# Streaming encoder step: input norm and the first three projections, interleaved block by block in five PSUM banks, with the bias rows spread once

## The chip, the core and the metric

The kernel runs on one core of a Trainium2 chip. Five engines work side by side, each on its own queue in program order: TensorE (PE, matmuls; PEld is its weight load), VectorE (DVE), ScalarE (ACT), GpSimd (POOL) and SyncE (SP), which here only issues DMAs. ACT issues DMAs too (its queue's rows are called ACTq). The metric is the device time of one execution in microseconds.

## What is computed

One inference step of two layers on 1024 prompt frames and 64 sample frames (1088 columns together), D = 1024. The part that matters is the start of layer 0: an RMS norm of the input and the first rows of the big input projection, for the first pair of attention heads.

```python
def rmsnorm(x, g):
    y = xf * lax.rsqrt(jnp.mean(xf * xf, axis=-1, keepdims=True) + EPS)
    return y * g
def mixer_even(h, conv_hist, ck, cv, w_in, conv_w, table, w_out):
    p = h @ w_in
    a_b, a_c, a_h, a_z, q, k, v, b_z = jnp.split(p, 8, axis=-1)
    ...
    o, nk, nv = band_attn_prompt(q, k, v, table)      # or band_attn_sample with the cache ck, cv
    ...
idx = jnp.clip(q_pos[:, None] - k_pos[None, :], -REL_CLIP, REL_CLIP) + REL_CLIP
bias = jnp.take(table, idx, axis=1)                   # added to the attention scores
```

## The kernel before

All activations lie transposed: channels on the 128 partitions in KT = 8 blocks, frames along the free axis in three groups of 384, 384 and 320 columns (`GROUPS`). Every fp32 product is made of three passes in a fast format: an operand is split into a rounded part `hi` (a copy on ACT) and the rest `lo` (a subtraction, mostly on DVE), and a projection adds w_hi·h_hi + w_hi·h_lo + w_lo·h_hi over the 8 blocks, so 24 matmuls for one weight tile and one group (`project`, line 174). The split weights are `whi`, `wlo` (`stage`, `split`, lines 147 to 164), the split normed input of group g is `hhi`, `hlo`. `project` writes one PSUM bank (`pjt`), taken from a pool of two by `bank`; an eviction (`ev_v`, `ev_q`, `ev_k`, `ev_z`) then copies it out.

`start` (line 353) does the input norm and the projections v, q, k (weights 0, 1, 2) of head pair 0. It squares the input blocks on ACT (line 377), adds the squares into `sqa` (line 379, on DVE for groups 0 and 1, on POOL for group 2), sums over partitions by one fp32 matmul with a constant (`rstd`, line 196), takes the root as exp(-0.5 ln) on ACT (lines 201, 202), and builds each normed block with three instructions (`h_tile`, lines 215 to 217): DVE makes `hf` = x · gain · rstd in SBUF, ACT rounds it to `hhi`, and DVE or POOL subtracts to get `hlo`. Group 0 is normed first. Then weight 0 runs over group 0; weight 1 over group 0, and the root of group 1 with its eight blocks; weight 2 over group 0, and the root of group 2 with its blocks. Groups 1 and 2 follow, weight by weight. A weight's tiles are given back by `drop` after its last group, which lets the next weight be staged; up to three are held. Below, "z" is the fourth projection of the pair (weight 3, line 654), and the first matmul of weight 4 follows it.

The bias table is needed as 128 shifted rows. `Lt` (line 639) is a short row for each of 8 heads, stored to DRAM as `Ld`; for each head `v_tokens` copies it 128 times to `Gd` (line 504) and reads it back at a slant as `bias` (line 506), all on ACT's DMA queue. The cached keys `ck` (line 445) share a buffer with the key output `ko` (tag "ko"), and are split in `split_k` directly after they are loaded (line 446).

What stands where in an engine's queue is decided at build time: the generators of `Order` set the order in which PE's work is written (`yield` lets attention units of a head pair in between), and the scheduler of the tile framework arranges each engine's instructions from that.

## Time and profile before

| what | us |
|---|---|
| median of 3 runs | 1475.85 (1473.38 to 1477.38) |
| the profiled execution | 1476.87 |
| its span, first to last instruction | 1475.1 |
| PE busy in the span | 1371.8 (93%) |
| DVE / ACT / POOL busy | 884.4 / 681.4 / 314.3 |
| mean granted TensorE clock | 0.98 |

Rows of a timeline give the start in us, the duration, the engine (ACTq and SPq rows are DMA issues), the line, the operation, out<-in, the shape, and in brackets how long the engine sat idle before it and what ended that. The duration of a matmul counts its way through the array, so that back-to-back matmuls overlap: their cost is the distance between starts. Rows of a window give for each engine the busy us and, in brackets, its number of instructions.

### The profile page before, as it was taken

Reading aid. Unit: us, or ns where it says so; the run is one execution under the profiler, and the core shown is the slowest. Engines: PE = TensorE matmul, PEld = TensorE weight load, DVE = VectorE, ACT = ScalarE, POOL = GpSimd, SP = SyncE. Lnnn points to the kernel's source line nnn. Section 1 sums busy time; section 2 is a strip of 40 time slices with the busy share of each in tenths; the row PEclk is TensorE's granted clock in tenths of the full one; section 3 lists DMA queues with packets and bytes.
Section 4 is the critical chain, followed back from the end, with each engine's and each line's share of the span. In section 5 each row is a group of like instructions: output and inputs, shape, how many; then the busy total and the mean of one; then the engine's idle time right before and its main releaser. Section 6 shows DMA issues by size and latency. Waiting matters only on the chain. (4 is left out here: it accounts for less than half of the span.)

```text
span 1475.1 us, 28417 instructions
## 1 busy us (share of the span) xinstructions
PE 1371.8 (93%) x10578; PEld 1233.6 (84%) x10578; DVE 884.4 (60%) x2496; ACT 681.4 (46%) x1780; POOL 314.3 (21%) x813
## 2 busy tenths in 40 slices
PE   4999999999999999989878999999999989998995
PEld 3888998999899899878867777878887877888985
DVE  6647237425624855768687767666766656443654
ACT  6544144234424446775455553544443534323642
POOL 4100000000000012341136224240424152210332
PEclk9999999999999999999999999999999999999998
DMA  5231210211121164551432222122211232347454
GB/s 204 63 136 44 78 59 26 78 61 45 53 70 58 34 216 137 181 186 60 85 98 69 40 43 61 35 42 48 70 33 41 61 87 70 92 122 229 150 188 157
DMA packets 114378, 133.12 MB, mean 90 GB/s; under 512 B 35568, under 2 KB 81336, under 8 KB 114240
## 3 DMA queue, kind: packets, MB, share of 16 engines
q1 hardware_dynamic: 82128, 101.86, 24.2%
q10 hardware_dynamic: 32112, 29.45, 6.1%
q8 instruction: 83, 1.36, 0.4%
q14 instruction: 55, 0.45, 0.1%
HBM read 99.91 MB, written 34.51 MB: 91 GB/s over the span
## 5 line engine op out<-in xcount | busy, mean ns | idle before, releaser
L119 PE MATMUL pjt<-hhi,wlo 128*128 128x384 f32 (+1 forms) x1768 | 620.8, 351 | 2.5 <-DVE wlo L164 2.4
L119 PE MATMUL pjt<-hhi,whi 128*128 128x384 f32 (+1 forms) x1768 | 586.7, 332 | 19.5 <-ACT whi L163 4.1
L119 PE MATMUL pjt<-hlo,whi 128*128 128x384 f32 (+1 forms) x1768 | 585.9, 331 | 7.3 <-DVE hlo L217 6.6
L119 PEld LDWEIGHTS pjt<-hhi,whi 128*128 128x128 f32 x1768 | 339.5, 192 | 29.5 <-ACT hhi L216 6.6
L119 PEld LDWEIGHTS pjt<-hhi,wlo 128*128 128x128 f32 x1768 | 339.9, 192 | 27.5 <-issue 12.4
L119 PEld LDWEIGHTS pjt<-hlo,whi 128*128 128x128 f32 x1768 | 338.4, 191 | 10.5 <-DVE hlo L217 8.8
L164 DVE TENSOR_TENSOR wlo<-wf,whi 128x512 fp32r<-128x512 f32 x222 | 155.8, 727 | 144.7 <-ACT whi L163 143.0
L163 ACT CAST whi<-wf 128x512 fp32r<-128x512 f32 x222 | 130.0, 619 | 160.5 <-PE pjt L119 113.0
L546 ACT ACTIVATE pr<-pr,mx 128x640 f32<-128x640 f32 (+5 forms) x72 | 50.9, 707 | 92.7 <-DVE mx L545 92.2
L721 DVE SCALAR_TENSOR_TENSOR kq<-pjt,par,kq 128x384 f32<-128x384 f32 (+2 forms) x144 | 71.6, 497 | 2.9
L347 POOL TENSOR_TENSOR sqa<-sqa,sq 128x384 f32<-128x384 f32 (+1 forms) x36 | 37.9, 1052 | 154.0 <-ACT sq L345 153.9
L507 POOL MEMSET bias<- 64x64 f32 x8 | 1.4, 178 | 313.1 <-DMA bias<-Gd 312.6
L543 DVE CUSTOM_DVE_ANT_0 pr<-sc,bias 128x640 f32<-128x640 f32 (+5 forms) x72 | 48.0, 666 | 26.3 <-PE sc L119 22.8
L928 POOL TENSOR_TENSOR px<-AL 48x14 f32<-48x14 f32 (+6 forms) x168 | 45.1, 269 | 61.3 <-DMA AL<-Sd 52.2
L1091 DVE SCALAR_TENSOR_TENSOR S<-S,egl,su 128x128 f32<-128x128 f32 x128 | 40.6, 343 | 28.9 <-PE su L119 28.5
L692 POOL TENSOR_TENSOR so<-so 128x4 f32<-128x4 f32 (+2 forms) x72 | 16.8, 233 | 176.7 <-DVE so L685 117.9
L882 ACT ACTIVATE junk<-tr 128x128 f32<-128x128 f32 x136 | 37.7, 277 | 34.9 <-PE tr L124 29.5
L929 POOL TENSOR_TENSOR AL<-AL,px 48x14 f32<-48x14 f32 (+6 forms) x168 | 46.7, 278 | 9.4
L119 PE MATMUL pjt<-mhi,whi 128*128 128x384 f32 x128 | 43.9, 343 | 4.9 <-ACT mhi L163 4.9
L124 PE MATMUL pt<-cst,pr 128*128 128x128 f32 (+1 forms) x280 | 43.2, 269 | 4.4 <-DVE pr L548 2.9
L1050 ACT ACTIVATE junk<-o 128x128 f32<-128x128 f32 x68 | 21.0, 309 | 51.9 <-DVE o L1046 43.1
L119 PE MATMUL pjt<-mlo,whi 128*128 128x384 f32 x128 | 43.9, 343 | 0.0
(238 smaller groups left out, 2208.5 us busy)
## 6 DMA issues: line engine op xcount, KB each, us to landing
wf<-in_w_in SPq DMA_DIRECT2D x128, 256.0 KB, 3.3
wf<-in_w_out SPq DMA_DIRECT2D x96, 256.0 KB, 3.3
mf<-mixd SPq DMA_DIRECT2D x32, 192.0 KB, 3.2
x<-in_x SPq DMA_DIRECT2D x8, 384.0 KB, 5.4
xg<-in_x SPq DMA_DIRECT2D x2, 1536.0 KB
xd<-xg SPq DMA_DIRECT2D x2, 1536.0 KB, 6.9
Dd<-dbuf ACTq DMA_DIRECT2D x16, 192.0 KB, 2.7
od<-o ACTq DMA_DIRECT2D x12, 256.0 KB, 3.4
```

The costliest lines, as they stand in the source:

```text
L119: return self.pe.matmul(out, lhsT=lhsT, rhs=rhs, start=start, stop=stop, **k)
L124: return self.pe.transpose(out, in_, self.ident[0:k, 0:k])
L163: self.act.copy(out=hi, in_=x)
L164: (eng or self.dve).tensor_tensor(lo, x, hi.bitcast(F32), ALU.subtract)
L347: pool.tensor_tensor(acc, acc, sq, ALU.add)
L543: dve.tensor_tensor_reduce(out=cut(pr[0:nq, :nk]), in0=sc[0:nq, :nk // nw, :nw], in1=cut(b["bias"][a][0:nq, j0:j0 + nk]), scale=1.0, scala ...
L546: act.activation(pr[0:nq, :nk], pr[0:nq, :nk], AF.Exp, bias=mx[0:nq, 1:2], scale=1.0, accum_out=mx[0:nq, 2:3])
L721: dve.scalar_tensor_tensor(oi, ch(ps[:, i0 + j + 1:i0 + j + 1 + m]), cw[j], oi, ALU.mult, ALU.add)
L882: act.activation(junk, ps[:, i, :], AF.Square, accum_out=ss[:, a, i0 + i:i0 + i + 1])
L928: pool.tensor_tensor(t, AL[:, j + 1:16, j:j + 1].broadcast_to([lanes, m, w]), x.broadcast_to([lanes, m, w]), ALU.mult)
L929: pool.tensor_tensor(o, o, t, ALU.add)
L1091: dve.scalar_tensor_tensor(Sn[:, q, :], S[:, q, :], egl[:, q, p, c:c + 1], su[q], ALU.mult, ALU.add)
```

## The change

`start` is written anew. Its parts, with their names in the diff:

- **Root.** Group 0's eight blocks are squared half on ACT and half on DVE, added in pairs, and the five remaining tiles go through five accumulating fp32 matmuls (`root`). Groups 1 and 2 are squared on ACT, and added on POOL except for the last square, which PE adds. The root goes back into the same PSUM tile (`rr`, one buffer) instead of SBUF, and `hf` lies in PSUM too (two buffers). All `hlo` are made on DVE.
- **Order.** One loop over the groups and, inside, over the 8 blocks: a block is normed some blocks ahead, then all three weights are applied to it (nine matmuls), into three banks at a time out of five. In group 2 only weights 0 and 1 run so, and weight 2 follows as a `project`. The squares of group g+1 are made during the first four blocks of group g, and its root is taken with the sixth.
- **PE fill.** Three fp32 matmuls on constants (`idle`) at the start, two more behind group 0's root; nobody reads them.
- **Staging.** Weights 0 and 1 use the permanent three buffers `wf`, weight 2 two buffers of its own; `cst` is loaded after the input.
- **Bias rows.** `Lt`, `Ld` and all eight `Gd` copies are issued on SP after group 0, `Lt` in the memory of group 0's input.
- **Cached keys.** `ck` has a buffer of its own, is loaded one step earlier for the later pairs, and is split before z.
- The PSUM pools of the attention are opened only after `start`.

```diff
-        return p.tile([P, 512], F32, name="pjt", tag="pj", bufs=2 if p is self.pj else 4)
+        return p.tile([P, 512], F32, name="pjt", tag="pj", bufs=2 if p is self.pj else self.extra)
...
-            wf = (tp if tp and len(self.ready) > 1 else self.wp).tile([P, 4, cols], F32, name="wf", tag="wf", bufs=3)
+            own = not tp or len(self.ready) < 2
+            wf = (self.wp if own else tp).tile([P, 4, cols], F32, name="wf", tag="wf", bufs=3 if own else 2)
...
     def start(self, evs, load):
...
+        pn = self.open("pn", space=PSUM)
+        self.more_banks(3, (0, 1, 0, 1, 1))
...
+        def root(g, parts):
+            n = GROUPS[g][1]
+            ps = pn.tile([P, 512], F32, name="rr", tag="rr", bufs=1)[:, :n]
+            for i, a in enumerate(parts):
+                self.mm(ps, self.meanm, a, i == 0, i == len(parts) - 1)
+            r = tp.tile([P, GMAX], F32, name="rstd", tag="rstd", bufs=1)[:, :n]
+            act.activation(r, ps, AF.Ln, bias=self.eps, scale=1.0)
+            act.activation(ps, r, AF.Exp, scale=-0.5)
+            return ps
+        def block(g, k, r):
...
+            hf = pn.tile([P, 512], F32, name="hf", tag="hf", bufs=2)[:, :n]
+            dve.scalar_tensor_tensor(hf, xs[g][:, k, :], self.par[:, P_PRE + k:P_PRE + k + 1], r, ALU.mult, ALU.mult)
+            act.copy(out=hi[:, k, :], in_=hf)
+            dve.tensor_tensor(lo[:, k, :], hf, hi[:, k, :].bitcast(F32), ALU.subtract)
+        def idle(n):
+            for _ in range(n):
+                self.mm(warm[:, :GMAX], self.meanm, self.eps.broadcast_to([P, GMAX]))
+        warm = self.bank()
+        idle(3)
...
+        r = root(0, parts)
+        idle(2)
+        self.ahead(tp)
+        ws = [self.take() for _ in range(3)]
...
+        for _ in range(3):
+            g, k = todo.pop(0)
+            block(g, k, roots[g])
         for g, (t0, n) in enumerate(GROUPS):
+            hi, lo = self.hops(g)
+            m = 3 if g < 2 else 2
+            ps = [self.bank() for _ in range(m)]
             for k in range(KT):
+                if todo:
+                    block(*todo[0], roots[todo[0][0]])
+                    todo.pop(0)
+                if g < 2:
+                    for j in range(2 * k, min(2 * k + 2, KT)):
+                        sq = square(g + 1, j, "sq" if j else "sqa", 3 if j else 1)
+                        if j == 0:
+                            acc = sq
+                        elif j < KT - 1:
+                            pool.tensor_tensor(acc, acc, sq, ALU.add)
+                    if k == 5:
+                        roots[g + 1] = root(g + 1, [acc, sq])
+                        todo = [(g + 1, i) for i in range(KT)]
+                        block(*todo.pop(0), roots[g + 1])
+                for w, p in zip(ws, ps):
+                    self.mm(p[:, :n], w[0][:, k, :], hi[k], k == 0, False)
+                    self.mm(p[:, :n], w[1][:, k, :], hi[k], False, False)
+                for w, p in zip(ws, ps):
+                    self.mm(p[:, :n], w[0][:, k, :], lo[k], False, k == KT - 1)
+            for i in range(m):
+                evs[i](g, ps[i])
                 if g == 2:
                     self.drop()
+            if g == 0:
+                Lt = tp.tile([8, LROW], F32, name="Lt", tag="x0")
...
+                    nc.sync.dma_start(self.Gd[h], bass.AP(row.tensor, row.offset, [[0, P], [1, LROW]]))
+        p = yield from self.project(ws[2], self.hops(2), GROUPS[2][1])
+        evs[2](2, p)
+        self.drop()
...
             def load():
-                ck = ap.tile([P, CB], F32, name="ck", tag="ko")
-                (nc.scalar if p else nc.sync).dma_start(ck, I["ckT"][p])
-                split_k(ck, [(SEQ, 0, CB)])
+                b["ck"] = ap.tile([P, CB], F32, name="ck", tag="ck")
+                (nc.scalar if p else nc.sync).dma_start(b["ck"], I["ckT"][p])
...
-                nc.scalar.dma_start(self.Gd[h], bass.AP(row.tensor, row.offset, [[0, P], [1, LROW]]))
...
                 if i == 1:
                     yield f"att{p - 1}.8"
                     new_qk()
+                    load()
                     load_v()
-                elif i == 3 and p:
-                    load()
+                elif i == 3:
+                    split_k(B[p]["ck"], [(SEQ, 0, CB)])
```

PE's queue at the first projection, before the change (whi_139 and wlo_140 are weight 0, hhi0 and hlo0 group 0's blocks, pjt_300 the bank):

```order
L119 MATMUL pjt_217<-sqa_194,mean_76 128x384
L119 MATMUL pjt_300<-hhi0_131,whi_139 128x384
L119 MATMUL pjt_300<-hlo0_132,whi_139 128x384
L119 MATMUL pjt_300<-hhi0_131,wlo_140 128x384
L119 MATMUL pjt_300<-hhi0_131,whi_139 128x384
L119 MATMUL pjt_300<-hlo0_132,whi_139 128x384
```

The same place with the change (whi_176, whi_186 and whi_196 are the three weights):

```order
L119 MATMUL rr_165<-s2_157,mean_76 128x384
L119 MATMUL pjt_131<-eps_73,mean_76 128x384 x2
L119 MATMUL pjt_231<-hhi0_159,whi_176 128x384
L119 MATMUL pjt_231<-hhi0_159,wlo_177 128x384
L119 MATMUL pjt_232<-hhi0_159,whi_186 128x384
L119 MATMUL pjt_232<-hhi0_159,wlo_187 128x384
L119 MATMUL pjt_233<-hhi0_159,whi_196 128x384
L119 MATMUL pjt_233<-hhi0_159,wlo_197 128x384
L119 MATMUL pjt_231<-hlo0_160,whi_176 128x384
L119 MATMUL pjt_232<-hlo0_160,whi_186 128x384
L119 MATMUL pjt_233<-hlo0_160,whi_196 128x384
```

Where one normed block fed three matmuls before the next one was needed, it now feeds nine, and `hlo` is asked for after six of them instead of after one.

ACT's queue between the last evictions of group 2 and z, before (Gd, bias and out_vT are DMA issues; whi is a weight's split):

```order
L504 DMA Gd_84<-Ld 128x767
L504 DMA Gd_85<-Ld 128x767
L474 DMA out_vT<-vT 128x576
L504 DMA Gd_86<-Ld 128x767
L453 ACTIVATE qs<-pjt 64x320 x2
L163 CAST whi<-wf 128x512
L506 DMA bias<-Gd_84 128x640
L506 DMA bias<-Gd_85 128x640
L163 CAST whi<-wf 128x512
L504 DMA Gd_87<-Ld 128x767
L504 DMA Gd_88<-Ld 128x767
L504 DMA Gd_89<-Ld 128x767
```

And with the change:

```order
L512 DMA vtok<-in_cv 128x4x128
L572 DMA bias<-Gd_84 128x640
L572 DMA bias<-Gd_85 128x640
L540 COPY vT<-pjt 128x320
L164 CAST whi<-wf 128x512 x2
L521 ACTIVATE qs<-pjt 64x320 x2
L164 CAST whi<-wf 128x512
L542 DMA out_vT<-vT 128x576
L504 CAST ks<-pjt 64x256 x2
L504 CAST ks<-pjt 64x64 x2
L164 CAST whi<-wf 128x512
```

The eight `Gd` issues are gone from ACT's queue (they stand on SP's, behind the weights that are prefetched), and only the two `bias` reads, which wait for `Gd`, are left ahead of the evictions.

ACT's queue in the middle of group 0, with the change (x_129 and x_130 are the inputs of groups 1 and 2; the whi in the middle is the second half of weight 1):

```order
L390 CAST hhi_159<-hf 128x384
L371 ACTIVATE sq<-x_129 128x384
L390 CAST hhi_159<-hf 128x384
L371 ACTIVATE sq<-x_130 128x320
L164 CAST whi<-wf 128x512
L390 CAST hhi_159<-hf 128x384
L371 ACTIVATE sq<-x_130 128x320
L390 CAST hhi_159<-hf 128x384
L504 CAST ks<-ck 64x512 x2
L508 COPY ks<-ks 64x512
L371 ACTIVATE sqa<-x_130 128x320
```

Squares of the next groups, a weight's split and the split of the cached keys stand between the blocks' roundings there.

## The prediction

> **What bounds the kernel now.** I read the page's head first, then windows cut at PE's own milestones, then the timeline of the first 90 us.

> ```profile
> PE 1371.8 (93%) x10578; PEld 1233.6 (84%) x10578; DVE 884.4 (60%) x2496; ACT 681.4 (46%) x1780; POOL 314.3 (21%) x813
> PE   4999999999999999989878999999999989998995
> ```

> PE is the bound nearly everywhere; the first of the 40 slices of PE is the weak one. The cuts below are the first projection matmul (15.03), the end of PE's longest early wait (30.66), the start of z (71.39) and the first matmul of weight 4 (88.60).

> ```profile
> 15.03:30.66 15.63, 8.89 (x19) 5.25 (x19) 15.48 (x20) 11.88 (x25) 10.03 (x9) 1.00 0.53 184
> 30.66:71.39 40.73, 37.37 (x201) 35.30 (x202) 23.33 (x42) 19.85 (x43) 6.44 (x7) 1.00 0.14 34
> 71.39:88.60 17.21, 13.74 (x75) 13.42 (x73) 4.47 (x9) 6.99 (x15) 0.58 (x4) 0.90 0.80 284
> 88.60:1475.10 1386.50, 1310.19 (x10286) 1179.16 (x10284) 832.22 (x2405) 632.27 (x1679) 294.21 (x788) 0.98 0.30 86
> ```

> In the second window DVE is busy 15.48 of 15.63 us: there it bounds, and PE does 19 matmuls. After 88.60 PE is busy 1310.19 of 1386.50, and its order of work there is the same with the change, row for row. So the case is decided by when the first matmul of weight 4 starts, plus what later stalls go or come.

> ```profile
> 15.03 0.69 PE L119 MATMUL pjt<-hhi,whi 128*128 128x384 f32 x1 [3.31 <-ACT hhi L216]
> 16.50 0.52 PE L119 MATMUL pjt<-hhi,whi 128*128 128x384 f32 x1
> 16.82 0.52 PE L119 MATMUL pjt<-hlo,whi 128*128 128x384 f32 x1
> 30.66 0.69 PE L119 MATMUL pjt<-hlo,whi 128*128 128x384 f32 x1 [4.63 <-DVE hlo L217]
> 35.95 0.40 PE L119 MATMUL pjt<-hhi,wlo 128*128 128x384 f32 x1
> 70.95 0.31 PE L119 MATMUL pjt<-hhi,whi 128*128 128x320 f32 x1
> 71.39 0.34 PE L119 MATMUL pjt<-hhi,whi 128*128 128x384 f32 x1
> 75.41 0.34 PE L119 MATMUL pjt<-hhi,wlo 128*128 128x384 f32 x1
> 79.22 0.44 PE L119 MATMUL pjt<-hhi,whi 128*128 128x384 f32 x1 [3.47 <-ACT ko L466]
> ```

> Matmuls overlap, so their price is the distance of starts. At 71.39 the 24 matmuls of z's first group take 23 distances in 4.02 us, 0.175 each; three of 320 columns take 0.44, 0.147 each. At 16.50 the same 384 columns take 0.32: PE runs at half pace. (The granted clock column says 1.00 there; the distances decide.)

> **Term 1, the first block: no gain.**

> ```profile
> 8.24 0.94 ACT L377 ACTIVATE sq<-x 128x384 f32<-128x384 f32 x2 [0.48 <-DMA x<-in_x]
> 10.07 1.65 PE L119 MATMUL pjt<-sqa,mean 128*128 128x384 f32 x2 [10.07 <-DVE sqa L379]
> 11.76 0.58 ACT L201 ACTIVATE rstd<-pjt,eps 128x384 f32<-128x384 f32 x1
> 12.74 0.52 ACT L202 ACTIVATE rstd<-rstd 128x384 f32<-128x384 f32 x1
> 38.27 0.81 PE L119 MATMUL pjt<-sqa,mean 128*128 128x384 f32 x2
> ```

> The last input lands at 8.24. Now two squares of it and the adds follow one another to 10.0; with the change one square is on ACT and one on DVE, done at 8.8. But five fp32 matmuls take the root where one did (a row with x2 is one of them, 1.65 slow, 0.81 fast). Three can start from about 5.5. If the fill matmuls have brought PE to full pace, the last two end at 8.8 + 1.6 = 10.4; if not, five at 1.65 end at 5.5 + 8.3 = 13.8. I take 11.5, near the 11.76 of now. After the logarithm ACT's queue holds three weight roundings, the exponential and the first block: 0.58 + 3 × 0.62 + 0.52 + 0.51 = 3.5 us against 3.27 now (11.76 to 15.03). First block at 15.0, bounds 13.9 to 17.3.

> **Term 2, PE's own work up to z.** 144 matmuls at 0.175 and 72 at 0.147 are 25.2 + 10.6 = 35.8, four root matmuls at 0.81 are 3.2: 39.0. From 15.0 this is a floor of 54.0 for z, against 71.39. It holds if nine matmuls per block (1.6 us) cover what the others do per block.

> ```profile
> L216 ACT CAST hhi<-hf 128x384 fp32r<-128x384 f32 x16 | 8.1, 510 | 3.8 <-DVE hf L215 3.7
> L377 ACT ACTIVATE sq<-x 128x384 f32<-128x384 f32 x14 | 6.9, 516 | 2.0 <-DMA x<-in_x 0.9 <-DVE sqa L379 0.9
> L163 ACT CAST whi<-wf 128x512 fp32r<-128x512 f32 x14 | 8.5, 617 | 7.6 <-PE pjt L119 3.7 <-DMA Gd<-Ld 3.7
> L164 DVE TENSOR_TENSOR wlo<-wf,whi 128x512 fp32r<-128x512 f32 x14 | 10.0, 737 | 8.2 <-ACT whi L163 8.1
> L379 POOL TENSOR_TENSOR sqa<-sqa,sq 128x320 f32<-128x320 f32 x7 | 7.4, 1061 | 1.8 <-ACT sq L377 1.6
> L215 DVE SCALAR_TENSOR_TENSOR hf<-x,par,rstd x24: 537/612/1390, 13.5 to 59.9; 128x384 f32<-128x384 f32 x16, 128x320 f32<-128x320 f32 x8
> L217 DVE TENSOR_TENSOR hlo<-hf,hhi x40: 480/550/1203, 15.1 to 695.8; 128x384 fp32r<-128x384 f32 x26, 128x320 fp32r<-128x320 f32 x14
> L453 ACT ACTIVATE qs<-pjt 64x384 fp32r<-64x384 f32 x4 | 1.9, 486 | 6.0 <-PE pjt L119 5.9
> L456 DVE SCALAR_TENSOR_TENSOR qs<-pjt,qs 64x384 fp32r<-64x384 f32 x4 | 2.2, 555 | 9.1 <-ACT qs L453 9.1
> ```

> DVE per block: 0.61 + 0.55 = 1.16. ACT per block: a rounding and one or two squares, 1.0 to 1.5. POOL: six adds a group, 6.4 us against some 14. On average PE is the longest, but not by much, and the queues are in order. So I count waits one by one:

> - First block: `hlo` is behind two weight subtractions on DVE, some 1.6 us after `hhi`; six matmuls cover 1.0. Wait 0.6.
> - Fifth block: weight 1's second half is rounded only after six block roundings and nine squares: 14.5 + 15 × 0.51 = 22.2, and 0.62 + 0.7 later it is split, 23.5; PE is there at 15.0 + 0.6 + 4 × 1.6 = 22.0. Wait 1.2 or so.
> - First block of group 1: the root's chain (0.58, 0.52, 0.61, 0.51, with squares between: about 5 us) against three blocks, 4.7. With its `hlo`: 0.9.
> - Third and fourth block of group 1: ACT evicts v, q, k of group 0 first (seven pieces at 0.49, 3.4 us), DVE four pieces at 0.555 (2.2). Wait 1.1.
> - Root of group 2: it writes `rr`, which the last `hf` of group 1 still reads. Wait 0.5.
> - Group 2: DVE has 8 × (0.54 + 0.48) + 2.2 = 10.4 us, PE 48 × 0.147 = 7.1, and DVE starts some 2.5 earlier. Wait 1.1.

> Together 5.4; bounds nothing (every chain a little shorter than counted) and 11 (each twice as long). z starts at 59.4, bounds 53 to 66.

> One price rests on `hf` and the root being in PSUM.

> ```profile
> 44.62 1.00 POOL L217 TENSOR_TENSOR hlo<-hf,hhi 128x384 fp32r<-128x384 f32 x1 [10.10 <-ACT hhi L216]
> 44.64 1.39 DVE L215 SCALAR_TENSOR_TENSOR hf<-x,par,rstd 128x384 f32<-128x384 f32 x1
> 737.05 1.20 POOL L839 TENSOR_TENSOR dbuf<-cst,dbuf 128x384 f32<-128x384 f32 x1 [2.62 <-DVE dbuf L836]
> 737.50 1.27 DVE L721 SCALAR_TENSOR_TENSOR vt<-pjt,cwh,vt 128x384 f32<-128x384 f32 x2
> ```

> Beside a POOL instruction `hf` from SBUF took 1.39 where its median is 0.61; the same operation with one operand in PSUM (`pjt`) took 0.64 each beside a longer POOL instruction. I therefore take 0.61 for `hf`, though twelve POOL adds stand beside the blocks; stretched by 0.7 each, they would cost DVE 8.4 us, which is inside rival B. [...]

> **Term 3, z.** From 71.39 to 88.60 are 17.2 us, of which PE's work is 48 × 0.175 + 24 × 0.147 = 11.9. The other 5.3 are the hole from 75.41 to 79.22 and half pace behind it. The hole comes from ACT, which waits in its queue:

> ```profile
> 65.20 0.57 ACTq L504 DMA_DIRECT2D Gd<-Ld  x1
> 70.51 2.71 ACTq L506 DMA_DIRECT2D bias<-Gd  x2
> 73.26 0.62 ACT L163 CAST whi<-wf 128x512 fp32r<-128x512 f32 x1 [3.67 <-DMA Gd<-Ld]
> 75.46 0.76 ACT L434 CAST ks<-pjt 64x256 fp32r<-64x256 f32 x2 [1.58 <-DMA out_vT<-vT]
> 78.74 0.43 ACT L466 COPY ko<-pjt 128x320 f32<-128x320 f32 x1
> ```

> ACT is held until the `Gd` copies land, so k of group 2 is evicted late and z's second group has no bank. With the change the copies go out on SP after group 0, from about 30. Behind them on SP stand only weight loads from the second half of weight 4 on, needed after 77. The first copy now takes 5.3 us (issued at 65.20, the read that waits for it goes at 70.51), so they are there before 40; ACT reaches the reads after 50. What is late next at z is weight 3, split once group 2 has left its buffer: 0.43 + 2 × 0.62 + 0.7 = 2.4, covered by weight 2's 24 × 0.147 = 3.5. So z costs 11.9 and ends at 71.3: **17.3 us earlier** than 88.60 (bounds 11 to 24).

> **Term 4, the cached keys of pairs 1 to 3.**

> ```profile
> 212.24 1.26 ACT L434 CAST ks<-ck 64x512 fp32r<-64x512 f32 x2 [6.11 <-DMA ck<-in_ckT]
> 214.93 0.45 PE L119 MATMUL pjt<-hhi,whi 128*128 128x384 f32 x1 [1.71 <-DVE zb L482]
> ```

> In pair 1 ACT waits for `ck` with z's eviction behind it, and PE stands 1.7 us. With a buffer of its own, loaded early, this wait goes. In exchange the split (four pieces at 0.62 on ACT, and its subtractions on DVE) stands beside the last softmax of the pair before, where it can delay an exponential by 0 to 0.7, three times. I take 0.2 in all: 1.5 gained, bounds -0.4 and 1.7.

> Everything else I cost at nothing: POOL's `hlo` going to DVE is in the 1.16; `cst` loaded later is first needed after z; the later opening of the attention's banks waits for evictions that are over 10 us old by then.

> **Sum.** 17.3 + 1.5 = 18.8 off the profiled execution's 1476.87 (its span, the 1475.10 that the last window ends with, and 1.8 around it): **1458.1**. That execution lies 1.0 above the median of 1475.85.

> **Rivals.**

> A, PE alone sets the pace: no wait of the list is left. z starts at 54, ends at 66: 22.7 + 1.7 off, 1452.5. For it: averages per block are below 1.6. Against: the in-order queues above. 0.17.

> B, ACT and DVE set the pace: the list is 10 to 11 us, z ends at 77, 12 + 0.5 off, about 1464. For it: in the second window DVE bounded at 15.48 of 15.63 us. Against: its stretched instructions are gone. 0.16.

> C, SP holds the weights: eight copies and the store of `Ld` stand ahead of the weights, each waiting for the one before. If they last to 80, weight 4 is some 6 us late: 1464 to 1468. 0.04.

> D, slower: PE stays at half pace. All 216 matmuls and z at 0.32 (0.27 for 320 columns, in proportion), roots at 1.65: 15 + 46.1 + 19.4 + 6.6 + 5.4 = 92.5, and 21.8 for z give 114 against 88.6, so 1502. It is slower than now from some 120 slow matmuls on (17.3 / 0.145). For it: now half pace holds from 15.03 to 35.95, through gaps of 0.3 to 4.6. Against: from 30.66 on, without a gap, it ended within 5.3 us (at 35.95 the rows turn shorter), and at half pace a block takes PE 2.9 us, more than anybody else needs, so there would be no gaps. [...] 0.02.

> E, it does not do what it says: the waits move, and z starts where it did. Within 0.3% only if 17 us of waits turn up. 0.01.

> **How the numbers follow.** The forecast has 0.60 and spans 1455 to 1462. A and B fill the range to both sides with bounds of the terms: 1451 to 1466; C's far end, D and E are outside. Under 0.3% (4.4 us) a measurement of this kernel can hardly tell from no change. Faster 0.97, same 0.01, slower 0.02.

> **What would show it.** First `hhi` at 14 to 15.5; matmuls 0.175 apart from there on; z's first matmul near 59; no hole inside z; weight 4 near 71; no wait at `ck`. It is wrong if PE's waits before z exceed 11 us, if half pace lasts beyond the second block, or if a new wait on `wf` or `Gd` appears after z.

## The result, and the profile after

| | before | after |
|---|---|---|
| median of 4 runs each, us | 1475.78 (1473.38 to 1477.38) | 1451.82 (1450.93 to 1457.86) |
| ratio, 95% interval | | 0.9854 [0.9834, 0.9874] |
| the profiled execution, us | 1476.87 | 1450.93 |
| its span | 1475.1 | 1449.1 |
| first projection matmul | 15.03 | 14.32 |
| first matmul of z | 71.39 | 55.72 |
| first matmul of weight 4 | 88.60 | 67.58 |

The change is 24.0 us faster, 1.5%. The predicted 1458.1 was 6.3 us too slow. The measured median lies just inside the range of 1451 to 1466 (one of the four executions, 1450.93, lies below it) and outside the 1455 to 1462 that the forecast alone spans. Of the gain 21.0 us are there when weight 4 begins.

The head of the page after, PE's busy time and its row of 40 slices:

```profile
PE 1372.1 (95%) x10600; PEld 1233.9 (85%) x10600; DVE 877.6 (61%) x2497; ACT 678.0 (47%) x1776; POOL 312.9 (22%) x810
PE   8999999999999999899878999999899989998996
```

PE's busy time over the whole run is the same; the weak first slice has gone from 4 to 8. The windows after, cut at the first projection matmul, the first of group 1, the first of group 2, z and weight 4 (busy us and number of instructions per engine, granted clock, DMA share, GB/s):

```profile
14.32:30.02 15.70, 15.68 (x77) 14.65 (x78) 12.47 (x24) 14.17 (x32) 10.00 (x11) 0.89 0.68 233
30.02:44.14 14.12, 14.07 (x77) 13.15 (x77) 12.47 (x25) 8.71 (x20) 1.38 (x2) 1.00 0.79 213
44.14:55.72 11.58, 10.96 (x73) 10.55 (x73) 8.78 (x19) 8.39 (x19) 0.00 (x0) 1.00 0.33 105
55.72:67.58 11.86, 11.86 (x74) 11.86 (x73) 5.16 (x10) 6.90 (x15) 0.59 (x4) 1.00 0.48 159
67.58:1449.10 1381.52, 1309.81 (x10286) 1179.49 (x10284) 831.37 (x2405) 632.35 (x1679) 297.83 (x788) 0.98 0.29 86
```

In the first three windows PE is busy 40.7 of 41.4 us, where it was busy 46.3 of 56.4 between the same two matmuls before. z has no hole: 11.86 us, all busy. In the last window PE's work is what it was (1309.81 against 1310.19). But in group 0 ACT is busy 14.17 of 15.70, and the clock is 0.89; both are followed up below. The timeline of PE at that place:

```profile
14.32 0.44 PE L119 MATMUL pjt<-hhi,whi 128*128 128x384 f32 x1 [2.09 <-ACT hhi L390]
14.61 0.34 PE L119 MATMUL pjt<-hhi,wlo 128*128 128x384 f32 x1
14.78 0.34 PE L119 MATMUL pjt<-hhi,whi 128*128 128x384 f32 x1
...
15.94 1.33 PE L119 MATMUL pjt<-hlo,whi 128*128 128x384 f32 x3
17.07 0.52 PE L119 MATMUL pjt<-hhi,whi 128*128 128x384 f32 x1
17.39 0.52 PE L119 MATMUL pjt<-hhi,wlo 128*128 128x384 f32 x1
...
18.82 0.68 PE L119 MATMUL pjt<-hlo,whi 128*128 128x384 f32 x3
19.34 0.33 PE L119 MATMUL pjt<-hhi,whi 128*128 128x384 f32 x1
```

At 14.61 starts are 0.17 apart, at 17.07 they are 0.32 apart, from 18.82 on 0.173 again: one stretch at half pace, after PE had stood 2.09 us for the first block.

### The profile page after: what moved, and what is told of

It is laid out like the page before. It is cut to its first block, busy times and chain, and to the rows that moved or that the text cites. A ratio compares the mean times of both kernels' runs of the same rounds, so it can differ in the third digit from the quotient of the medians.

```text
span 1449.1 us, 28440 instructions
## 1 busy us (share of the span) xinstructions
PE 1372.1 (95%) x10600; PEld 1233.9 (85%) x10600; DVE 877.6 (61%) x2497; ACT 678.0 (47%) x1776; POOL 312.9 (22%) x810
## 5 line engine op out<-in xcount | busy, mean ns | idle before, releaser
L119 PE MATMUL pjt<-hhi,wlo 128*128 128x384 f32 (+1 forms) x1768 | 617.7, 349 | 1.5 <-DVE wlo L165 1.5
L119 PE MATMUL pjt<-hhi,whi 128*128 128x384 f32 (+1 forms) x1768 | 583.7, 330 | 5.8 <-ACT whi L164 2.4
L119 PE MATMUL pjt<-hlo,whi 128*128 128x384 f32 (+1 forms) x1768 | 576.1, 330 | 0.7 <-DVE hlo L391 0.6
L119 PEld LDWEIGHTS pjt<-hhi,wlo 128*128 128x128 f32 x1768 | 337.6, 191 | 25.6 <-issue 11.7
L119 PEld LDWEIGHTS pjt<-hhi,whi 128*128 128x128 f32 x1768 | 337.6, 191 | 12.4 <-ACT whi L164 3.7
L119 PEld LDWEIGHTS pjt<-hlo,whi 128*128 128x128 f32 x1768 | 335.6, 190 | 1.8 <-DVE hlo L391 1.8
L164 ACT CAST whi<-wf 128x512 fp32r<-128x512 f32 x222 | 129.6, 618 | 165.0 <-PE pjt L119 123.4
L119 PE MATMUL pjt<-mhi,whi 128*128 128x384 f32 x128 | 44.4, 347 | 3.7 <-ACT mhi L164 3.7
L119 PE MATMUL pjt<-mlo,whi 128*128 128x384 f32 x128 | 44.5, 348 | 0.3 <-DVE mlo L165 0.2
```

The costliest lines, as they stand in the source:

```text
L119: return self.pe.matmul(out, lhsT=lhsT, rhs=rhs, start=start, stop=stop, **k)
L164: self.act.copy(out=hi, in_=x)
```

## The experiments

Totals are ratios to the kernel before, run on the same chip; they have intervals of 3 to 6 us to each side. The profiles show more: starts of matmuls, each from one profiled execution. "Distance" is from the first projection matmul to z's first, and takes out when the input happened to arrive.

| kernel | first block | z | distance | weight 4 | ratio, 95% interval |
|---|---|---|---|---|---|
| before | 15.03 | 71.39 | 56.36 | 88.60 | 1 |
| after | 14.32 | 55.72 | 41.40 | 67.58 | 0.9854 [0.9834, 0.9874] |
| fill5 | 13.89 | 55.32 | 41.43 | 68.14 | 0.9863 [0.9831, 0.9895] |
| nofill | 14.97 | 55.96 | 40.99 | 69.17 | 0.9875 [0.9843, 0.9908] |
| sq_late | 13.81 | 55.19 | 41.38 | 67.54 | 0.9847 [0.9819, 0.9875] |
| w1_early | 13.41 | 54.58 | 41.17 | 67.22 | 0.9845 [0.9803, 0.9886] |
| hf_sbuf | 13.41 | 60.75 | 47.34 | 72.61 | 0.989 [0.985, 0.993] |
| w_major | 13.55 | 65.58 | 52.03 | 77.42 | 0.9921 [0.9888, 0.9954] |
| root8 | 13.07 | 63.73 | 50.66 | 75.58 | 0.9907 [0.9871, 0.9943] |
| banks3 | 13.29 | 63.55 | 50.26 | 75.86 | 0.9912 [0.9885, 0.994] |
| gd_late | 14.11 | 55.48 | 41.37 | 73.88 | 0.9892 [0.9855, 0.9928] |
| gd_act | 13.77 | 56.15 | 42.38 | 68.31 | 0.9872 [0.9829, 0.9914] |
| only_gd | 15.96 | 72.62 | 56.66 | 84.56 | 0.9969 [0.9949, 0.9989] |
| ck_old | 13.74 | 55.14 | 41.40 | 67.04 | 0.9872 [0.9839, 0.9905] |

### Half pace and what fills it: fill5, nofill, sq_late, w1_early

**fill5**: five fill matmuls after group 0's root.

```diff
-        idle(2)
+        idle(5)
```

> Five fill matmuls behind group 0's root instead of two: they end near 14.0 instead of 12.2, so the idle stretch ahead of the first block (2.09 us in the changed kernel) nearly goes. Theory 1, the half-pace stretch from 15.16 to 18.58 comes from that idle stretch and costs 1.6 us of PE time: no half pace in group 0, the first matmul of weight 4 at 66.0 instead of 67.58. Theory 2, behind it the blocks themselves set the pace (in the changed kernel weight 1's second half was split at 22.40, just as PE wanted it at 22.46): the half pace goes, but waits of about 1 us come in its place, weight 4 at 67.0 to 67.6. By neither does the median move by more than 2 us.

Up to z theory 2 holds: PE no longer stands before the first block and the half pace is gone (starts are 0.17 to 0.19 apart from 14.17 on), and still the distance is 41.43. The timeline of PE in fill5 shows what stands in its place, at the fifth block:

```profile
20.83 0.33 PE L119 MATMUL pjt<-hhi,whi 128*128 128x384 f32 x1
21.01 0.34 PE L119 MATMUL pjt<-hhi,wlo 128*128 128x384 f32 x1
21.32 0.45 PE L119 MATMUL pjt<-hhi,whi 128*128 128x384 f32 x1
22.05 0.45 PE L119 MATMUL pjt<-hhi,wlo 128*128 128x384 f32 x1 [0.28 <-DVE wlo L165]
```

Six matmuls that take 1.04 us elsewhere take 1.85: weight 1's second half is late, as the prediction had it. Weight 4 lost the lead again inside z, where PE stood 0.7 us for an eviction (DVE's `zb`); at 68.14 it is later than either theory said, and why that eviction was late is open.

**nofill**: no fill matmuls at all (and the order of the banks adapted).

```diff
-        warm = self.bank()
-        idle(3)
...
-        idle(2)
```

> No fill matmuls at all. Theory 1, the fill is what has PE at full pace for the root and for most of group 0: five root matmuls at half pace, the logarithm near 13 instead of 11.36, PE at half pace until some 5 us into group 0, weight 4 at 70 to 71, 3 us slower. Theory 2, half pace in the first blocks is hidden behind waits for the blocks: weight 4 within 1 us of 67.58.

Group 0's root ran at half pace (four of its matmuls in 5.49 us, where those of group 1's root in the changed kernel start 0.64 apart), the first block came at 14.97, and half pace lasted to 17.9. The distance is even 0.4 shorter, z only 0.24 later than in the changed kernel. But the two z's can't be compared as they stand, because the input landed earlier here. ACT's last square of group 0 and the logarithm, in the changed kernel and then in nofill, with PE's root in nofill:

```profile
8.80 0.52 ACT L371 ACTIVATE sq<-x 128x384 f32<-128x384 f32 x1 [1.17 <-DMA x<-in_x]
11.36 0.58 ACT L381 ACTIVATE rstd<-rr,eps 128x384 f32<-128x384 f32 x1
```

```profile
7.35 0.52 ACT L371 ACTIVATE sq<-x 128x384 f32<-128x384 f32 x1 [0.68 <-DMA x<-in_x]
11.70 0.58 ACT L381 ACTIVATE rstd<-rr,eps 128x384 f32<-128x384 f32 x1 [1.29 <-PE rr L119]
5.34 5.49 PE L119 MATMUL rr<-sq,mean 128*128 128x384 f32 x8 [5.34 <-DVE sq L406]
```

From the last square to the logarithm are 4.35 us without fill, and 2.2 to 2.6 us in the eleven traces of the changed start with it. Counted from the last square, z comes 1.7 us later than in the changed kernel (48.61 against 46.92 us). So the fill is worth up to some 1.7 us up to z when the input lands early. When it lands as late as in the changed kernel, an estimate from these rows leaves 0.3 us: a root at half pace would have ended at about 11.7 there too. Weight 4 at 69.17 lies in neither theory's range; 1.1 us of its delay are a wait inside z for z's eviction (DVE's `zb`), and that the missing fill leads to that wait was not shown.

**sq_late**: fill5, and in the code the squares of the next group one step later.

```diff
-                    for j in range(2 * k, min(2 * k + 2, KT)):
+                    for j in range(max(0, 2 * k - 2), min(2 * k, KT)):
```

> The changed kernel with five instead of two matmuls that only fill time after group 0's root (as in the earlier run with five, which took away the half pace and got a wait of 1.85 us at the fifth block in its place), and with the squares of the next group one step later (squares 0 and 1 at the second block instead of the first, and so on). Theory 1 (the wait at the fifth block is ScalarE's order: the cast of weight 1's second half stood behind squares that wait for POOL's sums at 1.08 us each): the cast begins at 19 us or earlier instead of 20.7, the wait at the fifth block falls under 0.7 us, and z begins at 53.8 to 54.6 us instead of 55.3 with the five alone and 55.7 in the changed kernel, weight 4 about as much earlier. Theory 2 (the second half of weight 1 comes off the queue of loads too late anyway): the cast waits for its load, and z stays at 55 or above. Rival on the cost side: the root of the next group comes later (POOL's chain of six sums ends 1 us later), and TensorE waits 0.5 to 1 us at the sixth block.

It told nothing of its theory. The scheduler put ACT's instructions in the same order as in fill5, so weight 1's cast stayed at 20.56 and the distance at 41.38. It is a second run of fill5, and shows how well the distance repeats: within 0.05 us.

**w1_early**: fill5, and a buffer of its own for weight 1's second half (`rstd` gives up its place).

```diff
-            own = not tp or len(self.ready) < 2
+            own = not tp or len(self.ready) < 1 or (len(self.ready) == 1 and k == 0)
-            ... bufs=3 if own else 2)
+            ... bufs=3)
-            r = tp.tile([P, GMAX], F32, name="rstd", tag="rstd", bufs=1)[:, :n]
+            r = tp.tile([P, GMAX], F32, name="rstd", tag="s2", bufs=2)[:, :n]
```

> The changed kernel with five fill matmuls after group 0's root, and with a buffer of its own for the load of weight 1's second half (in the changed kernel this sixth half waits for a free buffer: it is issued at 12.9 us, behind seven reads of the next groups' input, and lands at 20.5; the cast follows at 21.1). Theory 1 (that load is the wait at the fifth block, which the run with five fill matmuls showed in place of the half pace): it lands before 14.5 us, the wait of 1.85 us at the fifth block is gone, the first block's second part comes 0.7 us later since one more weight remainder stands ahead of it on VectorE, and z begins at 53.6 to 54.8 us; weight 4 at 65.5 to 67.2 instead of 67.6. Theory 2 (VectorE's pace of 1.16 us a block, or POOL's sums for the next group's root, end as late): the wait moves to the blocks two to four or to the start of group 1, and z stays at 55 or above.

z's 54.58 lies where theory 1 wanted it, but only because this execution's first block came 0.9 us earlier than in the changed kernel. The fifth block's wait is gone (1.03 us for its six matmuls), group 1 begins 14.58 after the first block instead of 15.32 in fill5, and yet the distance is 41.17: 0.26 gained of 0.74. Theory 2 holds. The wait moved to the third block of group 1, and that block is the key to all four runs. Its `hlo` was ready, after the first block of group 0:

```
after 20.15   fill5 20.18   sq_late 20.14   gd_late 20.13   ck_old 20.15   w1_early 19.93   nofill 19.74
```

Each time PE took it 0.05 us later, and reached z 21.24 us after it. The timeline of ACT and DVE in the changed kernel ahead of it:

```profile
29.87 0.48 ACT L540 COPY vT<-pjt 128x384 f32<-128x384 f32 x1
30.62 0.97 ACT L521 ACTIVATE qs<-pjt 64x384 fp32r<-64x384 f32 x2
31.61 0.97 ACT L504 CAST ks<-pjt 64x384 fp32r<-64x384 f32 x2
32.61 0.86 ACT L390 CAST hhi<-hf 128x384 fp32r<-128x384 f32 x2
33.49 1.05 ACT L508 CAST ks<-ks 64x384 fp32r<-64x384 f32 x2
33.92 1.02 DVE L391 TENSOR_TENSOR hlo<-hf,hhi 128x384 fp32r<-128x384 f32 x2
```

Group 0's evictions stand ahead of the third and fourth block in ACT's row, without a gap. Up to that `hlo` ACT and DVE set the pace, whatever PE does at half or full pace before; this is why a stretch at half pace cost nothing before z. ACT's row holds more than evictions there: squares that wait for POOL's sums, and the split of the cached keys, from 23.35 to 26.41, directly ahead of group 1's logarithm, whose sum PE had done by 25.5. Whether that block comes earlier with the split elsewhere was not tried.

### Where the operands lie: hf_sbuf

```diff
-            act.activation(ps, r, AF.Exp, scale=-0.5)
-            return ps
+            act.activation(r, r, AF.Exp, scale=-0.5)
+            return r
...
-            hf = pn.tile([P, 512], F32, name="hf", tag="hf", bufs=2)[:, :n]
+            hf = tp.tile([P, GMAX], F32, name="hf", tag="s2", bufs=2)[:, :n]
```

> The changed kernel, with the root and the normed block in SBUF as before the change instead of in PSUM; the same instructions otherwise. Theory 1 (the place of the operands matters, term 2's 0.61 us): beside POOL's sums of squares VectorE's product of a block (hf) takes 1.3 us as in the kernel before, a block costs VectorE 1.9 instead of 1.17 us and, with six or seven blocks of each of the groups 0 and 1 in POOL's company, TensorE waits in group 0 and at the starts of the groups 1 and 2: weight 3's first matmul (z) at 58 to 60 us instead of 55.7, weight 4's at 70 to 72 instead of 67.6. Theory 2 (the slack of 0.5 to 5 us per block takes it): hf is longer, but z stays within 1 us of 55.7. [...]

Theory 1, a little beyond its range (z at 60.75, weight 4 at 72.61): the distance grows by 5.9 us. The 24 products of start, first after the change, then in hf_sbuf (min/median/max in ns):

```profile
L389 DVE SCALAR_TENSOR_TENSOR hf<-x,par,rr x24: 546/614/623, 13.1 to 49.7; 128x384 f32<-128x384 f32 x16, 128x320 f32<-128x320 f32 x8
```

```profile
L389 DVE SCALAR_TENSOR_TENSOR hf<-x,par,rstd x24: 547/610/1366, 12.1 to 54.7; 128x384 f32<-128x384 f32 x16, 128x320 f32<-128x320 f32 x8
```

With the root in PSUM none of the 24 was stretched beside POOL's adds (623 ns at most); with both inputs in SBUF six of them took 868 to 1366. The subtraction that makes `hlo` reads `hf` too: four of its 24 took 1.2 to 1.4 us, where none took over 0.56 after the change. Together DVE was stretched by 6.6 us, and POOL's six sums for group 1 took 1.2 to 1.9 us each instead of 1.0. The start of this trace has no half pace (starts are 0.17 to 0.18 apart from 13.69 on). The waits of PE in hf_sbuf's first 75 us (total, times, longest):

```profile
PE pjt L119 <- DVE hlo L391: 3.7, 5, 1.2
PE pjt L119 <- ACT hhi L390: 1.7, 1, 1.7
PE pjt L119 <- ACT whi L164: 1.6, 1, 1.6
```

### The order, the root's place, the banks: w_major, root8, banks3

**w_major**: the loops over the weights and the blocks change places; each weight runs through all eight blocks, and the blocks of the next group are normed beside the last weight.

```diff
-            for k in range(KT):
-                ...
-                for w, p in zip(ws, ps):
-                    self.mm(p[:, :n], w[0][:, k, :], hi[k], k == 0, False)
+            for i in range(m):
+                for k in range(KT):
+                    ...
+                    self.mm(ps[i][:, :n], ws[i][0][:, k, :], hi[k], k == 0, False)
```

> The changed kernel with the weights of a group one after the other (three times 24 matmuls) instead of all three by block; the blocks of group 0 are then all wanted within weight 0's 24 matmuls, those of the groups 1 and 2 are normed beside the last weight of the group before. Theory 1 (block by block is what lets TensorE run while a group is normed): group 0's eight blocks come at VectorE's pace of 1.17 us from 14.3 us on, so weight 0 ends near 24.5 instead of after 24 x 0.173 = 4.2 us, and TensorE loses some 4 to 5 us there, less whatever the half pace of the clock took in the changed kernel: z at 58 to 60.5 us instead of 55.7, weight 4 at 70 to 72.5. Theory 2 (the order matters little, because what counts is that the norms have left the path and the weights are there): z within 1.5 us of 55.7.

**root8**:

```diff
-                    if k == 5:
+                    if k == 7:
```

> The changed kernel with the next group's root issued with the eighth block of a group instead of the sixth. Theory 1 (the place of the root covers ScalarE's Ln and Exp and the first block): the two matmuls of group 1's root then run at about 28.5 us instead of 24, and Ln, Exp, the product and the cast of the first block (some 3 us in a row) end at 31.5 to 33, while TensorE wants that block at 30.0: a wait of 1.5 to 3 us at the start of group 1, and 1 to 2.5 at the start of group 2: z at 58 to 61 us instead of 55.7. Theory 2 (the slack, or other waits that fall away for it, takes the delay): z within 1 us of 55.7.

**banks3**:

```diff
-        self.more_banks(3, (0, 1, 0, 1, 1))
+        self.more_banks(1, (0, 1, 0))
```

> The changed kernel with three PSUM banks for the projections instead of five; the program's order is the same. Each group then needs all banks of the group before. Theory 1 (the two extra banks let a group begin while the one before is still read out): at the start of group 1 the first matmuls into the second and third weight's banks wait for weight 1's evictions (ScalarE qs, VectorE qs and so on), 2 to 3 us there and 1.5 to 3 at group 2: z at 58.5 to 61 us instead of 55.7. Theory 2 (the evictions come quickly enough, the blocks set the pace anyway): z within 1 us of 55.7.

All three are clearly slower, and by more than either theory gave: distances 52.0, 50.7 and 50.3. The waits themselves are about of the size expected. PE's timeline in root8 (its starts of groups 0, 1 and 2):

```profile
13.07 0.44 PE L119 MATMUL pjt<-hhi,whi 128*128 128x384 f32 x1 [1.84 <-ACT hhi L390]
32.38 0.69 PE L119 MATMUL pjt<-hhi,whi 128*128 128x384 f32 x1 [3.44 <-ACT hhi L390]
51.27 0.47 PE L119 MATMUL pjt<-hhi,whi 128*128 128x320 f32 x1 [2.54 <-ACT hhi L390]
```

and in banks3, for VectorE's eviction of q:

```profile
32.14 0.66 PE L119 MATMUL pjt<-hhi,whi 128*128 128x384 f32 x1 [1.87 <-DVE qs L524]
51.58 0.39 PE L119 MATMUL pjt<-hhi,whi 128*128 128x320 f32 x1 [1.89 <-DVE qs L524]
```

Most of the rest is the clock. In each of these kernels some of the waits are followed by a stretch at half pace that is a multiple of 3.41 us: in root8 at 13.93 (3.41), 31.0 (6.83) and 51.5 (3.41), in banks3 at 31.81 (6.83) and 52.29 (3.41). Windows of 3.41 us in root8:

```profile
27.58:31.00 3.42, 1.35 (x8) 1.03 (x6) 1.76 (x4) 3.36 (x9) 3.18 (x4) 1.00 0.63 168
31.00:34.41 3.41, 2.03 (x6) 2.03 (x7) 3.35 (x7) 3.29 (x8) 1.73 (x2) 0.50 1.03 257
34.41:37.82 3.41, 3.41 (x12) 3.41 (x12) 3.09 (x7) 1.94 (x5) 0.00 (x0) 0.50 1.03 262
```

At 31.00 the clock halves, behind a window in which PE was busy 1.35 of 3.42 us; it comes back behind the one in which PE was busy throughout. In w_major, where PE waited for blocks again and again from 13.55 on, half pace lasted from 15.95 to 26.19 and came again at 39.84. In root8 the two waits behind the first block are 6.0 us and half pace lasts 10.24 us longer than in the changed kernel, which is at most 5.1 us of PE's time; the distance grew by 9.3. w_major moves the norms of the groups 1 and 2 as well, so its 10.6 us are not the price of the order alone. Behind root8's waits of 3.44 and 2.54 us and banks3's of 1.87 and 1.89 us came half pace, 6.83 us of it behind the first of each pair and 3.41 us behind the second; from starts that are 0.32 apart in it instead of 0.175, an estimate puts its price at up to half of its length, 1.7 to 3.4 us on top of a wait.

### z and the bias rows: gd_late, gd_act, only_gd

**gd_late**: the changed kernel with `Lt`, `Ld` and `Gd` where and when they were before (on ACT, after `start`). **gd_act**: the copies early, but on ACT's queue. **only_gd**: the kernel before, with the early copies on SP alone.

```diff
+                    row = self.Ld[h:h + 1, :]
+                    nc.sync.dma_start(self.Gd[h], bass.AP(row.tensor, row.offset, [[0, P], [1, LROW]]))
...
-                nc.scalar.dma_start(self.Gd[h], bass.AP(row.tensor, row.offset, [[0, P], [1, LROW]]))
```

(the edit of only_gd, inside `start` and in `v_tokens`; gd_late undoes the same lines in the changed kernel, and gd_act puts `nc.scalar` for `nc.sync`, with the lines in the loop that reads the rows back.)

> The bias rows as before the change: short rows, store and the eight copies after the first projections, the copies on ACT's queue. Theory 1 (term 3 of the prediction): ACT is held by the copies, a hole of 3 to 4 us and half pace behind it come back inside z, weight 4 at 72 to 73 instead of 67.58, 5 us slower. Rival: the hole had its cause in the late evictions of the old start, and with the new start z still takes 11.9: no change.

> The changed kernel with the eight copies of the bias rows at the same early time, but issued from ScalarE's queue as in the kernel before; they then stand in ScalarE's row between the casts of group 1's blocks, at 0.33 to 0.6 us each, some 3 to 5 us in all. Theory 1 (term 3 is time, not queue: what counts is that the copies are done before z): no hole in z; the copies delay group 1's casts by up to 3 to 5 us, of which TensorE sees what exceeds the slack of 0.5 to 4 us per block: z at 56.5 to 60 us, weight 4 at 11.9 us behind it. Theory 2 (ScalarE's queue itself is the hole): z becomes 13 us long or more again.

> The kernel before, with one part of the change alone: the bias rows are read and copied after weight 0 of group 0, on SP's queue, as the changed kernel does it. Theory 1 (term 3: the bias copies made z 17.2 us long instead of 11.9): z begins at 71 to 72 us as before and weight 4's first matmul comes at 83 to 84 instead of 88.6; the total is about 1470.5. It is also a second look at the old way of loading ck: if the 1.7 us wait at pair 1's z belongs to that way, it is there again. Theory 2 (the copies only move and delay SP's weight loads, or the gain shows only together with the rest): weight 4's first matmul stays above 86.5 us.

gd_late's z begins with the distance of the changed kernel, and then has the old hole. PE, and ACT in whose row it arises:

```profile
63.65 0.34 PE L119 MATMUL pjt<-hhi,wlo 128*128 128x384 f32 x1
68.72 0.41 PE L119 MATMUL pjt<-hhi,whi 128*128 128x320 f32 x1 [4.73 <-DVE zb L541]
68.97 0.33 PE L119 MATMUL pjt<-hlo,whi 128*128 128x320 f32 x1
```

```profile
61.80 0.83 ACT L499 CAST ks<-ks 64x256 fp32r<-64x256 f32 x2 [3.23 <-DMA Gd<-Ld]
```

z costs 18.4 us instead of 11.9, with half pace behind the hole (320 columns 0.27 apart from 69.36 to 72.03, 0.15 from 72.56 on); weight 4 is 6.3 us later, a little more than theory 1 gave. In only_gd z begins late, as before, and takes 11.94: weight 4 at 84.56, 4.0 earlier than before although its z began 1.2 later; 5.3 of z's 17.2 us are gone. So term 3 is shown from both sides. gd_act has no hole either (12.2 us for z): the time of the copies matters, not the queue, and ACT pays 1.0 us of distance for them.

### The cached keys: ck_old

```diff
-                b["ck"] = ap.tile([P, CB], F32, name="ck", tag="ck")
+                b["ck"] = ap.tile([P, CB], F32, name="ck", tag="ko")
...
-                    load()
                     load_v()
-                elif i == 3:
+                elif i == 3:
+                    if p:
+                        load()
                     split_k(B[p]["ck"], [(SEQ, 0, CB)])
```

> The cached keys of pairs 1 to 3 in the key output's buffer again, loaded just ahead of z. Theory 1 (term 4): a wait of 1.7 us of PE returns at z of pair 1, 1.7 to 1.9 us slower, and nothing at pairs 2 and 3. Rival: the splits' new place beside the softmax costs what the wait cost: no change.

Counted from weight 4's first matmul to the same later matmul, the changed kernel gains another 2.0 us over the kernel before at pair 1. But ck_old does not lose them. There ACT waits for the keys again, and PE does not. ck_old's rows at pair 1, then those of the kernel before ahead of the wait that the prediction quotes:

```profile
183.68 0.34 ACTq L536 DMA_DIRECT2D out_kT<-ko  x1
185.79 0.35 ACTq L515 DMA_DIRECT2D ck<-in_ckT  x1
188.38 1.26 ACT L504 CAST ks<-ck 64x512 fp32r<-64x512 f32 x2 [3.82 <-DMA ck<-in_ckT]
```

```profile
205.24 0.34 ACTq L468 DMA_DIRECT2D out_kT<-ko  x1
209.36 0.35 ACTq L445 DMA_DIRECT2D ck<-in_ckT  x1
```

In both the load of the keys waits until the store of `ko` has left the buffer: 2.1 us in ck_old, 4.1 us before. With 2.1 ACT's wait is 3.82 instead of 6.11, and z's 24 matmuls cover it. only_gd, which loads in the old way, had 4.1 and a wait of PE of 1.5. At the pairs 2 and 3 it was 2.1 in all three. So the old way costs PE something only where that store lands late, which it did at pair 1 in both profiles of the old kernel's body and not in this one. What made it late stays open, and that the buffer of its own brought the 2.0 us is not shown.

## Why the prediction was right, and what in it was wrong

- **What bounds the kernel.** Right: 21.0 of 24.0 us are there at weight 4's first matmul, another 2.0 at pair 1. The experiments take apart the order, the root's place, the banks and the operands' place; what it is worth that the sums of squares left DVE was not tested by itself.
- **Term 1**, first block at 15.0: it came at 14.32, and the logarithm at 11.36 where 11.5 was taken. That this is so near was in part luck, because "no gain" was wrong: the last square began at 8.80 where the prediction had the input at 8.24. From the first square of the last input to the first block are 5.1 to 5.7 us in the eleven traces of the changed start with fill, and 6.7 to 6.8 in the two of the old one (before, only_gd), so the new root gains 1.1 us or more, and in the profiled pair the later input hid almost half of it. Between executions the first block moves by 1.2 us (13.07 to 14.32 with fill) with the landing of the input.
- **Term 2**, PE's floor of 39.0 between first block and z: the distance is 41.40, so 2.4 where the list of waits came to 5.4. This is the step that was off, by its size: 3.0 of the 3.7 us by which z was early (the rest is term 1). Single items: the first block 0.2 instead of 0.6 (fill5 shows 0.6); the fifth block nothing instead of 1.2 (fill5 shows 0.8, once half pace no longer delays PE); group 1's first block nothing instead of 0.9, since its `hhi` was ready 0.54 us early: ACT's chain from `Ln` at 26.41 to the rounding's end at 29.48 took 3.1, where 5 were counted; the third and fourth block of group 1 about 0.45 instead of 1.1; `rr` nothing instead of 0.5; group 2 1.1 as counted (the item's own figures, 10.4 - 7.1 - 2.5, give 0.8). Half pace, some 1.6 us, was not on the list and stood in rival D alone, and the two roots took 1.3 and 1.2 us where the floor has 1.6 each.
- The list's deeper fault was to **add waits along two chains as if they were one**. fill5 and w1_early take away 0.4 and 1.1 us of PE's delay before group 1 and get back 0.0 and 0.2, since the third block of group 1 is paced by ACT and DVE. Delays of PE ahead of it are not added, they are hidden.
- **`hf` at 0.61 from PSUM** was right and is worth 5.9 us of distance (hf_sbuf). The prediction put 8.4 us of stretching against it; 6.6 us of stretching came in hf_sbuf.
- **Term 3**, z at 11.9: 11.86, no hole. gd_late and only_gd show the cause.
- **Term 4**, 1.5: 2.0 came, but with the old way of loading ck_old did not lose it. The wait was read rightly from the profile; that it belongs to the shared buffer alone was not right, since the store's landing decides. That the number was nearly met does not confirm the cause.
- **Costed at nothing.** Right within what can be seen: weight 4 and pair 1 make 23.0 of the medians' difference of 24.0. The profiled pair differs by 26, but behind weight 4 single executions drift: w1_early is 0.4 us ahead of the changed kernel there and 5.9 behind it at the end, over the same instructions. For this reason the experiments were judged by milestones.
- **Rivals.** A's time (1452.5) is nearer to what came than the forecast, but not by A's reason: it had PE alone at 39.0, and 41.4 is ACT's and DVE's pace in the first half. B named those engines with four times their price. C: the copies were issued on SP from 28.1 us on, and no weight was late. D: half pace lasted 3.4 us.

## What to carry to other kernels

Interleaving weights by block pays through slack (here 0.5 to 5 us between a block's readiness and its use), so the place where two in-order queues meet evictions sets the pace; find that place before adding up waits, because delays ahead of it do not add. A DMA whose completion an engine waits for in its queue belongs early: here that was worth 5 to 6 us without touching the work, and a queue on which nothing waits behind it another 1.0 (gd_act). And a wait can cost more than its length, through the clock: banks3's two of 1.87 and 1.89 us were followed by 10.24 us at half pace, up to 5.1 us of PE's time by the same estimate, while the changed kernel's 2.09 us ahead of group 0, with 3.41 us at half pace behind them, cost nothing before z, since ACT's and DVE's chain hid them.

## What the runs showed of the hardware

```profile
11.75:15.16 3.41, 1.32 (x7) 0.84 (x6) 3.11 (x6) 3.41 (x9) 0.00 (x0) 1.00 1.06 376
```

```profile
28.40:31.81 3.41, 1.64 (x8) 1.01 (x7) 3.01 (x6) 3.03 (x8) 1.85 (x3) 1.00 0.79 214
```

and in two that were not, in gd_act and in hf_sbuf:

```profile
10.91:14.32 3.41, 1.70 (x7) 0.94 (x6) 2.83 (x6) 3.41 (x8) 0.00 (x0) 1.00 1.06 378
```

```profile
10.13:13.54 3.41, 1.67 (x6) 0.70 (x5) 2.85 (x6) 3.25 (x8) 0.00 (x0) 1.00 1.05 387
```

Behind 1.64 busy us the clock halved and behind 1.67 it did not; in w_major it halved behind 1.94 (the window at 36.43), and in the changed kernel it stayed at 1.00 behind 1.60 (at 1322.47), so these rows show no sharp line. The changed kernel's wait of 2.09 us ahead of the first block lies in one window, and half pace followed; in the kernel before, a wait of 2.18 us that ended at 1426.23 is shared by two windows, in which PE was busy for 2.17 and 2.03 us, and the granted clock stayed at 1.00. The start with two fill matmuls ran at half pace in the changed kernel's trace (1.32 busy us in the window at 11.75) and without it in gd_act's (1.70 in the one at 10.91), whose code is the same up to there.
